# Seven-product units in both FFNs of a two-layer decoder trunk, with the down groups moved between up groups

## The chip, the core and the metric

The kernel runs on one core of a Trainium2 chip. A core has a matrix engine (TensorE, "PE" in the profile; its weight loads are "PEld"), a vector engine (VectorE, "DVE"), a scalar engine (ScalarE, "ACT"), GpSimd ("POOL") and SyncE ("SP", which here only issues DMAs). Each engine works through its own instructions in the order in which the program emitted them; semaphores make one wait for another. The metric is the device time of one execution in microseconds, as the median of several runs.

## What is computed

One sequence of 256 tokens of width 2048 goes through two layers in float32. Layer 0 has a causal pooling mixer, layer 1 a mixture of three dilated causal attentions; each is followed by a gated feed-forward network (FFN) whose up-projection passes a causal convolution of width 3. What matters here is the FFN, which both layers have:

```python
D_FF = 5504          # 43 blocks of 128

def conv_ffn(h, w_up, conv_w, conv_b, w_down):
    S = h.shape[1]
    u = h @ w_up                                   # (256, 2048) x (2048, 11008)
    up = jnp.pad(u, ((0, 0), (CONV_WIDTH - 1, 0), (0, 0)))
    c = conv_b + up[:, 0:S] * conv_w[0]
    for j in range(1, CONV_WIDTH):
        c = c + up[:, j:j + S] * conv_w[j]
    gate, val = jnp.split(c, 2, axis=-1)
    return (jax.nn.silu(gate) * val) @ w_down      # (256, 5504) x (5504, 2048)

# in each layer
h = layer_norm(ALPHA * h + mix, ln1_g[i], ln1_b[i])
ff = conv_ffn(h, ffn_w_up[i], ffn_conv_w[i], ffn_conv_b[i], ffn_w_down[i])
h = layer_norm(ALPHA * h + ff, ln2_g[i], ln2_b[i])
```

## The kernel before

**Precision.** Every large product is made of three with rounded operands: a value x is split into a high part (rounded to float32r) and a low part (the rest), and h·h, h·l and l·h are added up. The weights are split on the chip: ScalarE copies the high part (line 82), VectorE subtracts it to get the low part (line 83).

**Units.** The work is a list `units`. A unit is a block of weights, 512 x 512 as a rule (1 MB), with the function that multiplies it and one that follows it (`post`). `run_units` takes them in order. At step i it first loads ahead (`do_load`, three raw buffers) and splits ahead up to unit i+3 (`SP_AHEAD = 3`, four buffers each for high and low parts); then it emits the matmuls of unit i, then the functions whose turn has come (`later(n, fn)`: n steps from now), then the unit's own `post`. So on VectorE and ScalarE the split of unit i+3 stands ahead of what follows unit i.

**Two layouts.** In the feature-major form (`group`, `mm_quad`, lines 149 to 182) the weights are stationary and 256 tokens stream past, high and low part side by side: 16 pairs of a 512-column matmul (line 164) and a 256-column one (line 165). In the token-major form (`group_tm`, lines 188 to 268) 128 tokens are stationary and 512 columns of weights stream past: 24 matmuls (lines 230 to 232). The residual stream is feature-major in `H`; layer 1 moves it to token-major `HT` before its FFN (`to_tokens`, line 703: a transpose of 32 x 32 blocks on VectorE, then 16 DMAs for each quad of features, issued by SP).

**Seven-product units.** Some token-major units use a Strassen-like scheme: the 512 x 256 by 512 x 512 product is cut in two in each direction, and seven block products take the place of eight. Such a unit is two entries in the list, "a" (three products) and "b" (four). `split_sums` splits the block for "a", then VectorE replaces the four quarters of the raw block by their sums and differences (lines 105 to 108); for "b" ScalarE copies the changed block (line 95) and VectorE subtracts (line 96). The sums of the other operand come from `left_sums` (line 619). Products that belong to more than one quarter of the result are left in two more PSUM banks (`s2`, `s3`); `early_post` adds them up on VectorE and puts them onto `HT` with accumulating DMAs from GpSimd (line 260).

**The FFN** (`ffn`, line 556). The hidden width is cut into quads of 512 features, q = 0 to 10 (the last has 384), and these into four chunks: 0 to 2, 3 to 5, 6 and 7, 8 to 10. For each q `up` appends a gate group and a value group, four units each. After a group `evac` adds the two halves of each bank (lines 579, 580); one step later `conv` makes the first tap and the bias on ScalarE (line 588) and two taps on VectorE (line 592, eight instructions for four blocks); then come the sigmoid and the products, and the split of the result `gq[q]`. When a chunk's quads are through, `down` appends its four down groups, one for each 512 columns of the output, each with a unit for each q. FFN 0 is feature-major (`resid_add` adds to `H`; the last chunk goes through `add_last`, which also makes the layer norm's statistics). FFN 1 is token-major, and eleven of its units are seven-product units: q = 1 and q = 4 in all four groups, q = 7 in one, q = 9 in two.

Of the kernel before, what the change touches and what calls it, by code (L numbers as in the profile page):

```python
# [9 lines left out]
F32 = mybir.dt.float32  # L10
# [22 lines left out]
def trunk(ctx: ExitStack, tc: tile.TileContext, x, pool_w_in, pool_w_grp, pool_scale, pool_w_out,  # L33
# [154 lines left out]
    def group_tm(w, r0s, c0, ncol, xqs, post, apart=False, seven=None, early=None):  # L188
# [5 lines left out]
        def mk_seven(kind):  # L194
            fin = len(r0s) == 2

            def go(h, l):
                if kind == "a":
                    ps.extend([bank("s2"), bank("s3")])
                x = xqs[1]()  # L200
# [4 lines left out]
                def sm(i):  # L205
                    return lambda hl, kk: seven()[i][:, hl, kk, :]


                if kind == "a":
                    prods = [(a(0, 0), 0, N1, 2, 0, True, False), (a(2, 0), 2, N1, 0, 0, False, False),  # L210
                             (sm(3), 2, N2, 0, 1, False, fin)]
                else:
                    prods = [(a(2, 1), 2, N1, 1, 0, False, fin), (sm(2), 0, N2, 3, 0, True, False),
                             (sm(0), 0, N1, 3, 1, False, True), (sm(1), 2, N2, 2, 1, False, True)]
# [40 lines left out]
        def done():  # L255
            if not apart:
                for t in range(2):
                    post(t, ps[t])
# [3 lines left out]
        for j, (r0, nr) in enumerate(r0s):  # L262
            src = w[r0:r0 + nr, c0:c0 + ncol]
            if seven is not None and j == 1:
                units.append((src, mk_seven("a"), None, "a"))
                units.append((None, mk_seven("b"), leave if j < len(r0s) - 1 else lambda: (leave(), done()), "b"))
                continue
# [33 lines left out]

    def resid_add(c, first):
        def post(ps):
            for m in range(4):
                y = H[c][:, m, :]
                if first:
                    V.scalar_tensor_tensor(y, y, ALPHA, ps[m][:, :T], op0=OP.mult, op1=OP.add)
                else:
                    V.tensor_tensor(y, y, ps[m][:, :T], OP.add)
            for m in range(4):  # L310
                y = H[c][:, m, :]
                V.tensor_tensor(y, y, ps[m][:, T:], OP.add)
        return post
# [146 lines left out]
    def add_resid(w, rows, srcs, first):  # L460
        for c in range(4):
            group(w, rows, 512 * c, 512, srcs, resid_add(c, first))

# [70 lines left out]
    def add_grp(g):  # L534
# [12 lines left out]
             True, 0, 0)  # L547
# [8 lines left out]
    def ffn(lay):  # L556
# [3 lines left out]
        sevens = {0: (1, (0, 1, 2, 3)), 3: (4, (0, 1, 2, 3)), 6: (7, (2,)), 8: (9, (0, 2))} if lay == 1 else {}  # L560
# [133 lines left out]
        for a, b in ((0, 3), (3, 6), (6, 8), (8, 11)):  # L694
            for q in range(a, b):
                up(q)
# [410 lines left out]
```

## Time and profile before

| what | before |
|---|---|
| median of 3 runs (lowest to highest) | 2061.21 us (2060.48 to 2064.47) |
| profiled execution: span | 2060.0 us |
| around the span, against the median | 1.2 us |
| TensorE busy | 2049.6 us, 99% |
| VectorE busy | 1505.6 us, 73% |
| ScalarE busy | 1032.9 us, 50% |
| TensorE clock granted, mean | 1.000 |
| loads of weights from HBM | 380.01 MB read |

In rows of groups ("L83 DVE TENSOR_TENSOR wl<-raw,wh 128x2048 ... x325 | 743.4, 2290 | ...") stand the source line, the engine, the operation, output and inputs, the shapes and the count; then the busy time of all together in us, the mean of one in ns, and the idle time of the engine just before them with what ended it. Instructions overlap a little on one engine, so busy time over count can be less than the mean. In rows of the timeline stand the start and the length in us, and in brackets how long the engine had idled and for what it had waited. In rows of windows stand the window, its length, and the busy time of each engine in it (with the number of instructions), then the clock, the share of the DMA engines and GB/s.

### The profile page before, as it was taken

What the parts mean: (1) busy time and instruction counts of PE and PEld (TensorE: products, weight loads), DVE (VectorE), ACT (ScalarE), POOL (GpSimd) and SP (SyncE); (2) the same over time, 40 slices, a digit from 0 to 9 for tenths busy, and PEclk for the clock granted to TensorE, in tenths of its full rate; (3) what the DMA queues carried; (4) which work ended last, traced back from release to release, by engine and by line L of the source; (5) the groups of instructions that cost most, each with busy time, mean ns of one, the idle gap of its engine ahead of it and who ended that gap; (6) DMA issues with size and microseconds to landing.
All of it is one profiled execution on the core that took longest, in us unless ns stands there. A gap on an engine that the chain in (4) does not pass through costs nothing.

```text
span 2060.0 us, 29055 instructions
## 1 busy us (share of the span) xinstructions
PE 2049.6 (99%) x11942; PEld 1799.5 (87%) x11942; DVE 1505.6 (73%) x1925; ACT 1032.9 (50%) x1139; POOL 36.5 (2%) x67
## 2 busy tenths in 40 slices
PE   9999999999999999999999999999999999999998
PEld 8999988888888888889888888998888888888887
DVE  6768877756756766779755667788886787676688
ACT  6445665345534535547544344575445544544552
POOL 2000000000000000000000000000010001000000
PEclk9999999999999999999999999999999999999999
DMA  8655565655555555555566555556686558556554
GB/s 269 212 189 189 173 197 172 203 184 185 184 196 191 171 198 180 182 183 172 191 193 200 174 169 179 179 180 186 190 253 219 189 164 265 184 164 222 166 184 164
DMA packets 236997, 393.71 MB, mean 191 GB/s; under 512 B 44878, under 2 KB 56292, under 8 KB 236608
## 3 DMA queue, kind: packets, MB, share of 16 engines
q1 hardware_dynamic: 231328, 385.52, 57.4%
q0 software_dynamic: 5104, 5.69, 1.7%
q8 instruction: 93, 1.52, 0.3%
q10 hardware_dynamic: 432, 0.66, 0.1%
q14 instruction: 40, 0.33, 0.0%
HBM read 380.01 MB, written 2.10 MB: 185 GB/s over the span
## 4 chain that ended last, share of the span: by engine, by line
PE 91%; DVE 4%; DMA 2%; ACT 1%; issue 1%; SPq 0%; POOL 0%; DVEq 0%; ACTq 0%; POOLq 0%
PE acc L164 47%; PE acc L165 24%; PE t L231 3%; PE t L230 3%; PE t L232 3%; PE acc L168 3%; PE acc L169 3%; PE acc L167 3%; DVE wl L83 1%; DMA raw<-in_ffn_w_up_dram 1%; ACT wh L82 1%; DMA raw<-in_ffn_w_down_dram 1%; DMA ht<-u 0%; ACT wh L95 0%; DVE wl L96 0%
## 5 line engine op out<-in xcount | busy, mean ns | idle before, releaser
L164 PE MATMUL acc<-xc,wh 128*128 128x512 f32 x3264 | 1149.5, 396 | 0.0
L83 DVE TENSOR_TENSOR wl<-raw,wh 128x2048 fp32r<-128x2048 f32 (+2 forms) x365 | 795.5, 2184 | 405.2 <-ACT wh L82 395.5
L82 ACT CAST wh<-raw 128x2048 fp32r<-128x2048 f32 (+2 forms) x365 | 664.2, 1825 | 535.5 <-PE acc L164 346.7
L165 PE MATMUL acc<-xc,wl 128*128 128x256 f32 x3264 | 915.9, 281 | 0.0
L164 PEld LDWEIGHTS acc<-xc,wh 128*128 128x128 f32 x3264 | 615.7, 189 | 145.7 <-DVE o L959 0.6
L165 PEld LDWEIGHTS acc<-xc,wl 128*128 128x128 f32 x3264 | 615.5, 189 | 0.2
L164 PE MATMUL acc<-g,wh 128*128 128x512 f32 x644 | 226.8, 396 | 0.0
L165 PE MATMUL acc<-g,wl 128*128 128x256 f32 x644 | 180.6, 280 | 0.0
L164 PEld LDWEIGHTS acc<-g,wh 128*128 128x128 f32 x644 | 121.5, 189 | 28.4
L592 DVE SCALAR_TENSOR_TENSOR c<-u,cv,c 128x256 f32<-128x256 f32 x344 | 141.6, 478 | 0.5
L165 PEld LDWEIGHTS acc<-g,wl 128*128 128x128 f32 x644 | 121.7, 189 | 0.0
L579 ACT COPY ut<-acc 128x256 f32<-128x256 f32 x164 | 58.8, 371 | 95.7 <-PE acc L165 95.4
L231 PE MATMUL t<-wl,g 128*128 128x512 f32 (+1 forms) x267 | 102.8, 385 | 0.3 <-DVE wl L83 0.3
L230 PE MATMUL t<-wh,g 128*128 128x512 f32 (+1 forms) x267 | 103.0, 386 | 0.0
L232 PE MATMUL t<-wh,g 128*128 128x512 f32 (+1 forms) x267 | 102.6, 384 | 0.0
L588 ACT ACTIVATE c<-u,cv 128x256 f32<-128x256 f32 x172 | 89.6, 596 | 3.1 <-DVE u L580 3.1
L580 DVE TENSOR_TENSOR u<-acc,ut 128x256 f32<-128x256 f32 x164 | 60.9, 416 | 30.7 <-ACT ut L579 30.7
L164 PE MATMUL acc<-o,wh 128*128 128x512 f32 x192 | 67.9, 396 | 0.0
L164 PE MATMUL acc<-mixed,wh 128*128 128x512 f32 x192 | 67.5, 395 | 0.0
L278 ACT CAST g<-c 128x1024 fp32r<-128x1024 f32 (+1 forms) x22 | 22.6, 1029 | 84.4 <-DVE c L658 84.4
L231 PEld LDWEIGHTS t<-wl,g 128*128 128x128 f32 x267 | 50.2, 188 | 11.1 <-DVE wl L83 1.1
L232 PEld LDWEIGHTS t<-wh,g 128*128 128x128 f32 x267 | 50.1, 188 | 11.0
(265 smaller groups left out, 2358.7 us busy)
## 6 DMA issues: line engine op xcount, KB each, us to landing
raw<-in_ffn_w_up_dram SPq DMA_DIRECT2D x160, 1024.0 KB, 5.1
raw<-in_ffn_w_down_dram SPq DMA_DIRECT2D x80, 1024.0 KB, 5.1
raw<-in_pool_w_out_dram SPq DMA_DIRECT2D x16, 1024.0 KB, 5.0
raw<-in_shared_w_k_dram SPq DMA_DIRECT2D x16, 1024.0 KB, 5.1
raw<-in_attn_w_q_dram SPq DMA_DIRECT2D x16, 1024.0 KB, 5.2
raw<-in_shared_w_v_dram SPq DMA_DIRECT2D x16, 1024.0 KB, 5.8
raw<-in_attn_w_o_dram SPq DMA_DIRECT2D x16, 1024.0 KB, 5.0
raw<-in_pool_w_in_dram SPq DMA_DIRECT2D x12, 1024.0 KB, 5.7
```

Of the source, the lines that this page charges most:

```text
L82: A.copy(wh[i][:, s], r[:, s])
L83: V.tensor_tensor(wl[i][:, s], r[:, s], wh[i][:, s].bitcast(F32), OP.subtract)
L164: PE.matmul(ps[m], h[:, k, c], q[:, k, :, :T], start=st, stop=False)
L165: PE.matmul(ps[m][:, :T], l[:, k, c], q[:, k, 0, :T], start=False, stop=sp and not shifted)
L167: PE.matmul(ps[m][:, :n], h[:, k, c], q[:, k, 0, :n], start=st, stop=False)
L168: PE.matmul(ps[m][:, :n], h[:, k, c], q[:, k, 1, :n], start=False, stop=False)
L169: PE.matmul(ps[m][:, :n], l[:, k, c], q[:, k, 0, :n], start=False, stop=sp and not shifted)
L230: PE.matmul(to, xh, h[:, k, c], start=j == 0 and k == 0, stop=False)
L231: PE.matmul(to, xh, l[:, k, c], start=False, stop=False)
L232: PE.matmul(to, xl, h[:, k, c], start=False, stop=j == len(r0s) - 1 and k == nk - 1)
L588: A.activation(c[:, m, :], u[:, m, 2:], AF.Identity, scale=cv[:, 2, j:j + 1], bias=cv[:, 3, j:j + 1])
L592: V.scalar_tensor_tensor(c[:, m, :], u[:, m, i:i + T], cv[:, i, j:j + 1], c[:, m, :], op0=OP.mult, op1=OP.add)
```

## The change

1. *Order.* A chunk's four down groups no longer stand together behind its up groups. For chunks 0 and 1 the order is: gate group of the next chunk's first quad, down group 0, its value group, down group 1, gate group of the second quad, down groups 2 and 3, its value group. For chunk 2: gate 8, down 0, value 8, down 1, gate 9, down 2, value 9, down 3. The last chunk's down groups stay at the end.
2. *Seven products.* In both layers q = 1, 2, 4, 5, 6 and 7 take seven block products in all four groups (q = 9 in two, in layer 1 only): 50 units where there were 11. A group of chunk 0 or 1 is then one plain token-major unit and two seven-product units, a group of chunk 2 two seven-product units. `mk_seven` now opens and closes its banks over several units; where all units of a group are seven-product units, only half of the second token block's bank is added up.
3. *FFN 0 is token-major in its first three chunks*: `to_tokens` follows its first layer norm; behind down group 3 of chunk 2 the new `to_features` brings each quad back (a transpose on VectorE, then two times eight DMAs on SP, three steps from quad to quad), and the last chunk is feature-major as before.
4. *Taps.* `conv` makes the other two taps on ScalarE as well, four instructions each, and VectorE adds each as one whole instruction. The product of gate and value moves from the third function to the second.
5. *Memory.* Evacuation tiles are two instead of four, the buffers of the left sums change, the attention masks are made later and in shared tiles.

```diff
-            for i in (1, 0):
+            a = pools["ffn"].tile([P, 4, T], F32, name="a", tag="t4")
+            for i, to in ((1, a), (0, u[:, :, 0:T])):
                 for m in range(nb):
                     j = blk0 + m
-                    V.scalar_tensor_tensor(c[:, m, :], u[:, m, i:i + T], cv[:, i, j:j + 1], c[:, m, :],
-                                           op0=OP.mult, op1=OP.add)
+                    A.activation(to[:, m, :], u[:, m, i:i + T], AF.Copy, scale=cv[:, i, j:j + 1])
+                V.tensor_tensor(c[:, :nb], c[:, :nb], to[:, :nb], OP.add)
...
             def tmp():
-                return fp.tile([P, T], F32, name="ut", tag="t1", bufs=4)
+                return fp.tile([P, T], F32, name="ut", tag="t1", bufs=2)
...
-        sevens = {0: (1, (0, 1, 2, 3)), 3: (4, (0, 1, 2, 3)), 6: (7, (2,)), 8: (9, (0, 2))} if lay == 1 else {}
+        chunks = [(0, 3), (3, 6), (6, 8), (8, 11)]
+        order = {0: (0, 1, 2), 3: (3, 4, 5), 6: (6, 7), 8: (8, 9, 10)}
+        every = (0, 1, 2, 3)
+        sevens = {1: every, 2: every, 4: every, 5: every, 6: every, 7: every}
+        if lay == 1:
+            sevens[9] = (0, 2)
+        wait = {}
...
-        for a, b in ((0, 3), (3, 6), (6, 8), (8, 11)):
-            for q in range(a, b):
-                up(q)
-            down(range(a, b), b == 11)
+        for q in range(3):
+            up(q, (), ())
+        for n in (0, 1):
+            d = down(n, False)
+            q = chunks[n + 1][0]
+            wait[q] = sum(len(g) for g in d[1:]) + 3
+            up(q, d[:1], d[1:2])
+            up(q + 1, d[2:], ())
+            if n == 0:
+                up(q + 2, (), ())
+        d = down(2, False)
+        wait[9] = len(d[3]) - 1
+        up(8, d[:1], d[1:2])
+        up(9, d[2:3], d[3:])
+        up(10, (), ())
+        mark = len(units)
+        if lay == 0:
+            rows = [(512 * q, min(512, FF - 512 * q)) for q in (8, 9, 10)]
+            add_last(w_dn, rows, [lambda q=q: gq[q] for q in (8, 9, 10)], False, 0, 1)
+            turns(mark, 3, 3)
+        else:
+            groups = down(3, True)
+            for g in groups:
+                units.extend(g)
+            turns(mark, len(groups[0]), len(groups[1]))
...
+    def to_features(c):
+        hb = hp.tile([P, 4, T], F32, name="hb", tag="h")
+        hf = hb.rearrange("p m t -> p (m t)")
+        V.transpose(hf.rearrange("p (m t c) -> p t m c", m=4, t=2), HT[c].rearrange("p t (m c) -> p t m c", m=4))
+
+        def move(part):
+            if part == 0:
+                H[c] = hp.tile([P, 4, T], F32, name="h", tag="h")
+            to = H[c].rearrange("p m t -> p (m t)").rearrange("p (k a j) -> p a k j", k=8, a=4)
+            fr = hf.rearrange("p (k b j) -> p b k j", k=8, b=4)
+            for a in (2 * part, 2 * part + 1):
+                for b in range(4):
+                    nc.sync.dma_start(to[32 * b:32 * b + 32, a], fr[32 * a:32 * a + 32, b])
+
+        later(1, lambda: move(0))
+        later(2, lambda: move(1))
```

More of the change, by code (lines that the diff above doesn't have):

```diff
@@ L694, in ffn @@
-        for a, b in ((0, 3), (3, 6), (6, 8), (8, 11)):
-            for q in range(a, b):
-                up(q)
-            down(range(a, b), b == 11)
+            for c in range(4):
+                sv = {j: (lambda q=q: xs[q]) for j, q in enumerate(qs) if c in sevens.get(q, ())}
+                group_tm(w_dn, rows, 512 * c, 512, srcs, tm_post(lay, n, c), apart=last and c == 3,
+                         seven=sv, early=early_post(c, not last))
+                groups.append(units[mark:])
+                del units[mark:]
@@ L744, in early_post, with tm_post @@
         return post
-    def tm_post(c, first, last):
+    def tm_post(lay, n, c):
         parts = [slice(0, 256), slice(256, 512)]
+        first, last = n == 0, n == 3
         def post(t, ps, half=None):
             y = HT[c][:, t, :]
+            if lay == 0 and n == 2 and c == 3 and t == 1:
+                for q in range(4):
+                    later(1 + 3 * q, lambda q=q: to_features(q))
             if half is None and first:
```

105 lines of the change are left out of this document (45 added, 60 removed).

## The prediction

> **What bounds the kernel now.** First the page: span, busy table, clock, chain. Then the windows of the two stages that already hold seven-product units, the matmuls' timeline (to price a unit), and the timelines of VectorE and ScalarE there.
>
> ```profile
> span 2060.0 us, 29055 instructions
> PE 2049.6 (99%) x11942; PEld 1799.5 (87%) x11942; DVE 1505.6 (73%) x1925; ACT 1032.9 (50%) x1139; POOL 36.5 (2%) x67
> PEclk9999999999999999999999999999999999999999
> PE 91%; DVE 4%; DMA 2%; ACT 1%; issue 1%; SPq 0%; POOL 0%; DVEq 0%; ACTq 0%; POOLq 0%
> ```
>
> TensorE is busy 99% of the span at full clock and is 91% of the chain. Only fewer matmul columns, or fewer pauses, can make the kernel faster; and any pause adds its full length. The profiled execution's span is 2060.0 us; the median of the runs is 2061.21, so 1.2 us lie around it.
>
> Windows of layer 1's down groups of chunks 0 and 1 (span, then busy time of PE, PEld, DVE, ACT, POOL, clock, DMA share):
>
> ```profile
> 1464.00:1530.00 66.00, 64.49 (x359) 55.19 (x358) 55.32 (x63) 33.38 (x31) 7.81 (x9) 1.00 0.69 211
> 1666.00:1731.00 65.00, 65.00 (x365) 56.41 (x364) 56.53 (x64) 32.18 (x29) 7.77 (x9) 1.00 0.70 216
> ```
>
> With one seven-product unit among three, VectorE is already 84 to 87% busy there, against 73% over the span, and in the first window TensorE loses 1.51 us. That is the stage to watch.
>
> **The gain: TensorE's own work.** An up unit is 16 pairs of lines 164 and 165. A token-major unit (T) is the run of lines 230 to 232; two stand between the first two starts below, and one seven-product unit (S, entries "a" and "b") between the last two.
>
> ```profile
> L164 PE MATMUL acc<-xc,wh 128*128 128x512 f32 x3264 | 1149.5, 396 | 0.0
> 1676.91 0.40 PE L230 MATMUL t<-wh,g 128*128 128x512 f32 x1
> ...
> 1688.08 0.28 PE L219 MATMUL s<-wh,g 128*128 128x256 f32 x1
> ...
> 1693.06 0.40 PE L230 MATMUL t<-wh,g 128*128 128x512 f32 x1
> ```
>
> Each line-164 matmul overlaps the next one's start, so its busy time over its count is the pair's pitch: 1149.5/3264 = 0.352 us, and an up unit, or a feature-major down unit, is 16 x 0.352 = 5.63. T is 11.17/2 = 5.585, S is 4.98. Seven-product units go from 11 to 50: 24 in FFN 0 replace feature-major ones (24 x 0.65 = 15.6 us), 15 in FFN 1 replace T (15 x 0.605 = 9.1), and 8 units of FFN 0 become T (8 x 0.045 = 0.4). Gain 25.1 us. The 1.51 us of pauses above would go as well, as that stage is rebuilt.
>
> **The price: VectorE.** One stretch of its timeline, then ScalarE's rows and the by-shape groups.
>
> ```profile
> 1677.28 2.29 DVE L83 TENSOR_TENSOR wl<-raw,wh 128x2048 fp32r<-128x2048 f32 x1 [0.58 <-ACT wh L82]
> 1679.49 1.82 DVE L103 TENSOR_TENSOR wl<-raw,wh 128x1024 fp32r<-128x1024 f32 x2
> 1681.23 0.68 DVE L105 TENSOR_TENSOR raw<-raw 128x512 f32<-128x512 f32 x1
> ...
> 1684.01 0.42 DVE L730 TENSOR_TENSOR w<-w,s 128x256 f32<-128x256 f32 x1
> ...
> 1686.13 2.29 DVE L96 TENSOR_TENSOR wl<-raw,wh 128x2048 fp32r<-128x2048 f32 x1 [0.46 <-ACT wh L95]
> 1688.34 2.28 DVE L83 TENSOR_TENSOR wl<-raw,wh 128x2048 fp32r<-128x2048 f32 x1
> 1690.54 1.28 DVE L754 TENSOR_TENSOR ht<-ht,t 128x512 f32<-128x512 f32 x2
> 1691.74 2.28 DVE L83 TENSOR_TENSOR wl<-raw,wh 128x2048 fp32r<-128x2048 f32 x1
> 1694.59 1.83 DVE L103 TENSOR_TENSOR wl<-raw,wh 128x1024 fp32r<-128x1024 f32 x2 [0.57 <-ACT wh L101]
> 1662.91 2.29 DVE L96 TENSOR_TENSOR wl<-raw,wh 128x2048 fp32r<-128x2048 f32 x1 [2.03 <-ACT wh L95]
> ```
> ```profile
> 1655.20 1.57 ACT L101 CAST wh<-raw 128x1024 fp32r<-128x1024 f32 x2 [2.27 <-PE acc L164]
> 1666.56 0.37 ACT L579 COPY ut<-acc 128x256 f32<-128x256 f32 x1 [1.04 <-PE acc L165]
> 1666.83 2.08 ACT L588 ACTIVATE c<-u,cv 128x256 f32<-128x256 f32 x4
> 1675.34 1.91 ACT L82 CAST wh<-raw 128x2048 fp32r<-128x2048 f32 x1
> ```
> ```profile
> L592 DVE SCALAR_TENSOR_TENSOR c<-u,cv,c 128x256 f32<-128x256 f32 x344 | 141.6, 478 | 0.5
> L610 DVE TENSOR_TENSOR c<-u,c 128x1024 f32<-128x1024 f32 x20 | 24.3, 1216 | 0.5 <-ACT u L609 0.5
> L641 DVE TENSOR_TENSOR xs<-f,xs 128x256 fp32r<-128x256 f32 x14 | 5.0, 417 | 0.0
> L396 ACT ACTIVATE xp<-h,vec 128x256 fp32r<-128x256 f32 x48 | 20.4, 498 | 0.0
> L580 DVE TENSOR_TENSOR u<-acc,ut 128x256 f32<-128x256 f32 x164 | 60.9, 416 | 30.7 <-ACT ut L579 30.7
> ```
>
> From start to start: a plain split 2.21; the "a" half of a seven split 1.74 + 2.78 = 4.52 (two low parts, four subtractions in place); its "b" half 2.21; the group's posts 1.66 + 1.20 = 2.9. Between "a" and "b" ScalarE must copy the changed block (1.91), which waits for "a" and lets VectorE idle 2.03 us when nothing stands between them, 0.46 when the posts do. A taps pair costs ScalarE 8 x 20.4/48 = 3.4 us (nearest row: line 396, a copy with a per-partition scale), after four of line 588 in 2.08: its conv lasts 5.5 us instead of 2.08. VectorE gives up eight taps of 141.6/344 = 0.41 (3.3 us) and gets two whole additions like line 610's, 2.4 us.
>
> Over the whole span this fits: VectorE 1505.6 - 44 convs x 0.9 + 39 units x 4.5 + nine further sets of left sums (eight operations of 0.42 each, 30 us) is about 1670 of 2060 us, ScalarE 1032.9 + 344 x 0.425 + 39 x 1.6 about 1240. But the average isn't what decides. Two rules in the code set how far the splits may run ahead: SP_AHEAD = 3, and four weight buffers, so entry i+4 is split only after TensorE has finished entry i. A seven unit is two entries, so a lead of three entries is only 7 to 11 us of TensorE there.
>
> A *down group of chunks 0 and 1* becomes T, S, S: TensorE 5.585 + 2 x 4.98 = 15.5 us; VectorE 2.21 + 2 x 6.73 + 2.9 = 18.6, and up to 4 us of waiting for ScalarE. An up group is 22.5 us of TensorE, and some 15 of VectorE (four splits 8.8, evacuation 1.5, conv 2.4, product 1.2, half a set of sums). An up and a down group together just fit, 34 to 38 against 38. One down group between two up groups I therefore cost at nothing: the lead covers it. But groups 2 and 3 of each chunk stand side by side. Zero is the end of the up group before them; two T and two S pairs, but for the last "b", end at 31.1 - 2.8 = 28.3 us without a pause. By zero VectorE has the first three entries' splits done. Until the last "b" is split it has left, in program order: three "a" 13.6, three "b" 6.6, one T 2.2, conv 2.4, sigmoid's product 1.2, posts 2.9: 28.9 us; before the first it waits 1.6 for ScalarE (evacuation, copy), 1.0 at the "b" behind the conv, and twice 2.0 at a "b" with nothing before it: 35.5. A pause of 7.2 us, four times (two chunks, two layers): 28.8. Lower bound: only the two 2.0-us waits, 4.6 each, 18. Upper: the 4 us of waits in both groups, 9 each, 36. I take the middle, since each wait has its row.
>
> A *down group of chunk 2* is S, S: 9.95 us of TensorE. Here ScalarE's order binds. At zero the up group ends; evacuation until 0.6, the "b" copy 1.9 (its buffer comes free at zero), the conv 5.5, only then the next up unit's copy 1.9, then VectorE 2.2: 12.1, and 12.8 when VectorE is still on the "a" before, since evacuation tiles fall from four to two. So 2.5 us of pause. The next three groups start without a lead: an up and a down group ask VectorE for 8.8 + 1.5 + 2.4 + 1.2 + 13.5 + 2.6 + 5 of waits = 35 in TensorE's 32.5, so they pause longer, 3.8 by the same sum carried on. 2.5 + 3 x 3.8 = 13.9 per layer, 27.8. Bounds: 2.1 each (17), 5 each (40).
>
> **The rest.** Moves between layouts are SP's:
>
> ```profile
> 1410.87 13.34 SPq L717 DMA_DIRECT2D ht<-hb  x16
> 1424.31 1.65 SPq L72 DMA_DIRECT2D raw<-in_ffn_w_up_dram  x3
> ht<-hb SPq DMA_DIRECT2D x64, 32.0 KB, 2.0
>   DMA ht<-hb: 1.3, 1
> L260 POOL DMA_DIRECT2D ht<-u x18: 1159/1337/1519, 1494.0 to 1859.1; - x18
> ```
>
> To tokens in FFN 0 stands among up groups, as it does in layer 1, where its only trace is VectorE's 1.3 us: nothing. Back to features, each quad's 16 moves hold SP 13.3 us, land 2.0 later, and the next quad's transpose on VectorE needs that buffer; it comes every three units, of 12 x 0.352 = 4.2 in the narrow group 10, so 12.7. With the load issues that blocks VectorE's queue, splits behind it, 0 to 6 us three times; the lead there is 12.7 us. I take 2 (0 to 18). Weight loads queue behind the moves on SP, at most half a quad (6.7 us) now. POOL gets 45 more accumulating DMAs of 1.3 us on an engine 2% busy: nothing, but a group's post waits for the last one's landing if it follows closely. Left sums lie in up groups; masks move to an up group; feature-major posts (line 312) and token-major posts cost VectorE alike: nothing each.
>
> Sum: 2061.2 - 25.1 - 1.5 + 28.8 + 27.8 + 2 = **2093 us**, slower by 1.6%. With all lower bounds 2070, with all upper ones 2129.
>
> **Rivals.**
> *Faster: the lead holds.* If ScalarE runs its conv and copies ahead of VectorE, no wait adds and the pauses of chunks 0 and 1 shrink to 28.9 - 28.3 = 0.6 us each. It decides where all pauses together fall under 26.6 us, less than half of my sum. For it: up and down groups fit on average. Against: the 2.03 and 0.57 us waits are there in an easier order. Without pauses 2034.6; with chunk 2's at their lower bound and chunks 0 and 1's at 0.6, 2054. I name 2045, chance 0.24.
> *No change.* The pauses eat the gain: 2057 to 2065, 0.04.
> *The clock falls in the pauses.* Here it never did:
>
> ```profile
> 2040.00:2052.00 12.00, 11.16 (x76) 9.24 (x74) 11.57 (x23) 1.72 (x4) 1.72 (x2) 1.00 0.26 59
> ```
>
> In this window TensorE idles most of a microsecond and the granted clock stays 1.00; no row has a pause of 4 us inside the work. If each of the ten pauses of 3.8 us or more were followed by half a unit at half rate, 2.8 us each, the time is 2093 + 28 = 2121. The Trainium skill, "TensorE: Matmul & The Clock Gate", Part 1, has the array's clock halve after an idle window of about 3.4 us until as long a busy one has passed; by it each such pause would cost, as an estimate, 1.7 us more, 17 in all. The trace neither agrees nor disagrees, for want of such a pause. Chance 0.04.
> *The way back to features chokes*: 18 instead of 2, 2109, chance 0.05.
>
> **How the numbers follow.** My forecast 0.63 (its own range 2070 to 2110), the rivals as above. About 0.2%, 4 us, is what a measurement can tell. The range 2043 to 2112 leaves out half of the faster case and the clock's. Faster 0.24, same 0.04, slower 0.72.
>
> **What would show it.** After: 132 matmuls of line 164's kind on g where 644 were, and 50 x 42 of the seven products; PE's busy sum lower by about 25 us; but idle time of PE some 60 us, released by VectorE's low parts: about 7 us in groups 2 and 3 of chunks 0 and 1 in both layers, 2 to 4 behind each down group of chunk 2, where VectorE in turn waits for ScalarE's copies behind the conv. Line 592 is gone. I am wrong if VectorE is dense there and TensorE yet has no pauses (then the splits lead by more than I think), or if pauses stand at loads or transposes instead.

## The result, and the profile after

The changed kernel takes 2163.66 us as the median of four runs, beside 2061.35 for the kernel before on the same chip: a ratio of 1.0495 (95% interval 1.0481 to 1.0510). It is 102 us slower, not 32 as forecast, and outside the range, which ended at 2112. The direction and the two mechanisms that the prediction priced are in the trace; two thirds of the loss are not among its terms.

From the page of the changed kernel: span, busy table, chain, and the mean clock from the view of cores.

```profile
span 2162.9 us, 30852 instructions
PE 2068.3 (96%) x12388; PEld 1834.3 (85%) x12388; DVE 1678.5 (78%) x1971; ACT 1236.1 (57%) x1612; POOL 75.3 (3%) x112
PE 54%; DVE 20%; ACT 15%; DMA 6%; issue 5%; SPq 1%; ACTq 0%; DVEq 0%
core 0: 2162.9 us, clock 0.981
```

TensorE, 91% of the chain before, is 54% of it now; VectorE and ScalarE have 35%, and DMAs 6%. The busy sums came out as forecast (VectorE 1678.5 against "about 1670", ScalarE 1236.1 against "about 1240"), and no engine but TensorE is busy more than 78% of the span. So the loss is in waits. TensorE's busy sum must not be read as work here: it grew by 19 us although there is less to multiply, and the 30.9 us by which slow clock stretched matmuls (table below) are part of that sum.

Where TensorE waited, from its waits (us in total, times, longest):

```profile
PE acc L165 <- DVE wl L83: 22.6, 11, 2.4
PE t L223 <- ACT wh L95: 22.4, 8, 4.0
PE t L224 <- DVE wl L96: 21.2, 14, 1.9
PE acc L164 <- ACT wh L82: 5.0, 9, 1.7
PE shift L361 <- DVE S L344: 4.9, 1, 4.9
```

All but the last of these are waits for a high or a low part of weights, thus for ScalarE's copies and VectorE's splits; the last is for a sum of the layer norm at the end of FFN 0. The prediction named L96 and L83. It did not name ScalarE's copy for a "b" (L95), at 22.4 us, as something that TensorE itself waits for.

A sum over the starts of all matmuls shows where the 102.9 us of span went. Each interval from one matmul's start to the next is set against the usual interval of its kind in the same trace; what exceeds it counts as clock when it lies in a stretch of half clock, else as a pause.

| us | before | after | difference | forecast |
|---|---|---|---|---|
| matmuls at their usual pitch | 2042.6 | 2017.0 | -25.6 | -25.1 |
| pauses | 12.8 | 111.1 | +98.3 | +57 |
| matmuls stretched at half clock | 0 | 30.9 | +30.9 | 0 |
| rest (jitter both ways) | | | -0.7 | |

The pauses by place, both layers together: groups 2 and 3 of chunks 0 and 1 27.7 (forecast 28.8); around the groups of chunk 2 22.7 (forecast 27.8); the start of chunk 1's up groups and the first down group of each chunk 37.7 (forecast 0); the rest stands at the end of FFN 0 (forecast 2) and where the kernel before paused too, as at its start and in layer 1's attentions.

### The profile page after: what moved, and what is told of

The parts are those of the page before. It is cut to its first block, busy times and chain, and to the rows that moved or that the text cites. A ratio compares the mean times of both kernels' runs of the same rounds, so it can differ in the third digit from the quotient of the medians.

```text
span 2162.9 us, 30852 instructions
## 1 busy us (share of the span) xinstructions
PE 2068.3 (96%) x12388; PEld 1834.3 (85%) x12388; DVE 1678.5 (78%) x1971; ACT 1236.1 (57%) x1612; POOL 75.3 (3%) x112
## 4 chain that ended last, share of the span: by engine, by line
PE 54%; DVE 20%; ACT 15%; DMA 6%; issue 5%; SPq 1%; ACTq 0%; DVEq 0%
PE acc L164 26%; PE acc L165 13%; DVE wl L83 5%; DMA raw<-in_ffn_w_up_dram 4%; ACT wh L95 3%; ACT wh L82 3%; ACT c L585 3%; DVE wl L103 3%; DVE wl L96 2%; PE acc L169 2%; PE acc L168 2%; PE acc L167 2%; ACT a L590 2%; DMA raw<-in_ffn_w_down_dram 2%; ACT u L590 2%
## 5 line engine op out<-in xcount | busy, mean ns | idle before, releaser
L83 DVE TENSOR_TENSOR wl<-raw,wh 128x2048 fp32r<-128x2048 f32 (+2 forms) x326 | 703.1, 2170 | 236.4 <-ACT wh L82 230.2
L95 ACT CAST wh<-raw 128x2048 fp32r<-128x2048 f32 x50 | 95.3, 1906 | 167.7 <-DVE raw L108 157.3
L96 DVE TENSOR_TENSOR wl<-raw,wh 128x2048 fp32r<-128x2048 f32 x50 | 114.6, 2292 | 73.0 <-ACT wh L95 68.9
L576 ACT COPY ut<-acc 128x256 f32<-128x256 f32 x164 | 56.6, 372 | 132.2 <-DVE u L577 120.5
L224 PE MATMUL t<-wl,g 128*128 128x256 f32 x296 | 87.8, 297 | 22.8 <-DVE wl L96 21.2
L223 PE MATMUL t<-wh,g 128*128 128x256 f32 x296 | 85.6, 289 | 22.4 <-ACT wh L95 22.4
L103 DVE TENSOR_TENSOR wl<-raw,wh 128x1024 fp32r<-128x1024 f32 x100 | 91.1, 953 | 11.2 <-ACT wh L101 11.2
L101 ACT CAST wh<-raw 128x1024 fp32r<-128x1024 f32 x100 | 78.5, 834 | 33.8 <-DMA raw<-in_ffn_w_down_dram 16.8
L223 PE MATMUL s<-wh,xs 128*128 128x256 f32 x300 | 89.9, 300 | 0.0
L224 PE MATMUL s<-wl,xs 128*128 128x256 f32 x300 | 89.5, 298 | 0.0
L225 PE MATMUL s<-wh,xs 128*128 128x256 f32 x300 | 89.1, 297 | 0.0
L225 PE MATMUL t<-wh,g 128*128 128x256 f32 x296 | 85.2, 288 | 0.0
L234 PE MATMUL t<-wh,g 128*128 128x512 f32 (+1 forms) x211 | 81.2, 385 | 0.6 <-ACT wh L82 0.6
```

Source lines behind the costliest of these rows:

```text
L83: V.tensor_tensor(wl[i][:, s], r[:, s], wh[i][:, s].bitcast(F32), OP.subtract)
L95: A.copy(h, r)
L96: V.tensor_tensor(l, r, h.bitcast(F32), OP.subtract)
L103: V.tensor_tensor(l[:, k, n], r[:, k, n], h[:, k, n].bitcast(F32), OP.subtract)
L223: PE.matmul(to, xh, h[:, k, n], start=opens and kk == 0, stop=False)
L224: PE.matmul(to, xh, l[:, k, n], start=False, stop=False)
```

## The experiments

All edits are to the changed kernel unless another is named. "Lost" is the time from a group's first matmul to the next group's first, less its units at their usual price; it holds pauses and slow clock together. Ratios are to the kernel before, with their 95% intervals.

**Is it the clock?** In 18 stretches inside the work, 3.4 or 6.8 us long, the clock was half. Unread matmuls were put into the pauses, or ahead of them, to keep TensorE busy. They change no result.

```diff
+    def fill(ps, n):
+        for _ in range(n):
+            PE.matmul(ps[:, :T], neg1, XC[0][:, 0, 0, :T], start=True, stop=True)
+# 14 to 40 of them ahead of the "b" entries that wait, 16 to 30 ahead of the up groups that wait
```

> The changed kernel with matmuls that nobody reads put in front of the entries where TensorE was seen to pause over 2 us: 14 to 40 of 256 columns (0.118 us each) at the first narrow group behind chunk 0's up groups, at the 'b' entries of down groups 0 and 3, and at the up groups behind chunk 2's down groups. They fill the pauses, but leave the waits. Theory 'clock': the 19 stretches at half clock (84 us, in which matmuls took some 31 us more) come from the pauses; with TensorE kept at work they go, and the time falls by 20 to 30 us, to about 2138. Theory 'waits only': the clock's dips cost nothing of their own or come from elsewhere; the time stays at 2163 or rises by what the added matmuls overrun, to 2175.

2163.0 us (1.0487, 1.0466 to 1.0508): the time stayed, while the mean clock rose from 0.981 to 0.992. The stretches at half clock fell from 82 to 34 us and the stretched matmuls from 30.9 to 15.2 us. The pauses fell from 111.1 to 64.2, that is by 47 us, but 58 us of unread matmuls were spent on that: some 11 us of them stood in no pause and were work added, which hides most of what the clock gave back. Matched matmul by matmul with the changed kernel, this run gained 1.4 to 2.4 us at each of the four groups 3 of chunks 0 and 1 (7.5 in all), where the unread matmuls stood in the pause and no stretch of half clock was left; elsewhere it gained and lost up to some 4 us at a place. So slow clock seems to cost time of its own at least in groups 3. How much of the 30.9 us of the table would go with the clock alone, this run does not settle, as half of the slow time remained.

**Are loads late behind the layout moves?** Every second move between the layouts goes to GpSimd's queue instead of SP's, in `to_tokens` and `to_features`.

```diff
-                    nc.sync.dma_start(...)
+                    (nc.sync, nc.gpsimd)[b % 2].dma_start(...)
```

> The changed kernel, and every second move between the layouts issued by GpSimd instead of SP; nothing else. Theory 'late loads': of the pauses that I had costed at nothing, those where chunk 1's up groups begin and in the down group behind them (6.0 + 8.9 us in layer 0, 3.5 + 10.9 in layer 1), and the end of FFN 0 (8 us), come from weight loads that wait behind moves on SP's queue; half of these 37 us or more go, 2130 to 2145. Theory 'q = 2's conv': they come from conv, products and left sums of q = 2 standing right before the group; only the end of FFN 0 gains, 2153 to 2160.

2134.62 us (1.0354, 1.0333 to 1.0375): 29 us gained. The stretch before the first down group of layer 0 shows how. First the changed kernel, one fence for each engine's timeline (SP, ScalarE, TensorE):

```profile
337.63 15.55 SPq L736 DMA_DIRECT2D ht<-hb  x16
353.28 1.48 SPq L72 DMA_DIRECT2D raw<-in_ffn_w_up_dram  x1
```
```profile
359.32 1.91 ACT L82 CAST wh<-raw 128x2048 fp32r<-128x2048 f32 x1 [6.70 <-DMA raw<-in_ffn_w_up_dram]
```
```profile
371.71 0.50 PE L164 MATMUL acc<-xc,wh 128*128 128x512 f32 x1 [1.70 <-ACT wh L82]
374.65 0.58 PE L165 MATMUL acc<-xc,wl 128*128 128x256 f32 x1 [2.43 <-DVE wl L83]
...
399.22 0.58 PE L223 MATMUL t<-wh,g 128*128 128x256 f32 x1 [3.95 <-ACT wh L95]
```

Then the same moves with the queue split (SP, GpSimd, ScalarE):

```profile
333.19 8.21 SPq L736 DMA_DIRECT2D ht<-hb  x8
```
```profile
333.73 4.61 POOL L736 DMA_DIRECT2D ht<-hb  x8 [11.26 <-DVE u L577]
```
```profile
347.47 1.91 ACT L82 CAST wh<-raw 128x2048 fp32r<-128x2048 f32 x1 [1.62 <-PE acc L164]
```

The 16 moves of one quad held SP for 15.55 us, the weights behind them came late, and ScalarE idled 6.70 us for a load; TensorE stood still only 10 to 40 us later, when the lead of three entries had been used up. With the queue split the copy waits for TensorE instead, that is, for a free buffer: the lead is whole. What was lost at the start of chunk 1's up groups went from 6.0 and 3.5 us (layer 0 and 1) to 0, in the first down group of chunk 0 from 8.9 and 10.9 to 3.8 each, at the end of FFN 0 from 8.0 to 1.8: 27.9 of the 29 us.

What was left in the first down groups, 3.8 us, has a row too. ScalarE's and VectorE's timelines of the run with the split queue, in the first down group:

```profile
380.97 2.09 ACT L585 ACTIVATE c<-u,cv 128x256 f32<-128x256 f32 x4
...
386.16 1.90 ACT L95 CAST wh<-raw 128x2048 fp32r<-128x2048 f32 x1
```
```profile
388.10 2.29 DVE L96 TENSOR_TENSOR wl<-raw,wh 128x2048 fp32r<-128x2048 f32 x1 [0.44 <-ACT wh L95]
```

The copy for the "b" stands behind the 5.2 us of the conv, its split ends at 390.4, and TensorE waits for it:

```profile
390.44 0.38 PE L224 MATMUL t<-wl,g 128*128 128x256 f32 x1 [1.95 <-DVE wl L96]
```

The next two runs take ScalarE's order apart.

**Is it ScalarE's taps?** First the two taps go back to VectorE.

```diff
-            for i, to in ((1, a), (0, u[:, :, 0:T])):
+            for i in (1, 0):
                 for m in range(nb):
                     j = blk0 + m
-                    A.activation(to[:, m, :], u[:, m, i:i + T], AF.Copy, scale=cv[:, i, j:j + 1])
-                V.tensor_tensor(c[:, :nb], c[:, :nb], to[:, :nb], OP.add)
+                    V.scalar_tensor_tensor(c[:, m, :], u[:, m, i:i + T], cv[:, i, j:j + 1], c[:, m, :],
+                                           op0=OP.mult, op1=OP.add)
```

> One part undone: the two other taps are VectorE's again, eight instructions of 0.41 us, no whole additions. VectorE gets 0.9 us more per conv (40 us in all), ScalarE 3.4 us less. Theory 'ScalarE's order': the pauses behind chunk 2's down groups (23 us in both layers) and at the first up group behind chunk 0 (4.6 and 3.4 us) come from a conv of 5.5 us standing before the next copy on ScalarE; they shrink to less than half and the time falls to 2125 to 2145. Theory 'VectorE's sum': VectorE's work as such sets the pauses; they grow by 10 to 20 us, and the time is 2170 to 2185.

2136.6 us (1.0359, 1.0338 to 1.0380): 27 us gained, in the range of the theory of ScalarE's order, although VectorE has more to do. In layer 0 the loss before chunk 1's up groups fell from 6.0 to 0.2, in the first down group of chunk 1 from 3.8 to 0, in chunk 2's first group from 5.9 to 1.4. In groups 2 and 3 it stayed (10.3 and 9.7, before 9.8 and 8.6), and in chunk 0's first group it rose from 8.9 to 10.7.

But the theory had the pauses behind chunk 2's down groups shrink to less than half, and they didn't: TensorE's idle time in the eight up groups there (both layers) was 19.6 us in the changed kernel and 17.3 here. VectorE's and TensorE's timelines of this run show why: the taps now stand on VectorE, ahead of the low part that TensorE waits for.

```profile
800.14 3.25 DVE L589 SCALAR_TENSOR_TENSOR c<-u,cv,c 128x256 f32<-128x256 f32 x8
...
804.56 2.28 DVE L83 TENSOR_TENSOR wl<-raw,wh 128x2048 fp32r<-128x2048 f32 x1
```
```profile
806.90 0.39 PE L165 MATMUL acc<-xc,wl 128*128 128x256 f32 x1 [3.23 <-DVE wl L83]
```

Second, the taps stay with ScalarE, but the last one, with the product behind it, is emitted one step later, so that copies can come between.

```diff
-            for i, to in ((1, a), (0, u[:, :, 0:T])):
-                ...
+            tap(c, u, cv, 1, pools["ffn"].tile([P, 4, T], F32, name="a", tag="t4"), blk0, nb)
+        # the caller, one step on:
+            later(1, half)      # half: last_tap(c, u, ...), the product, then later(..., three)
```

> The changed kernel with each conv spread over two steps: bias and first two taps in one, the last tap (and what follows) one step later, so that the next unit's copy on ScalarE waits for 3.8 us of conv instead of 5.5. No work is added or taken away. Theory 'ScalarE's order': the pauses behind chunk 2's down groups (23 us) fall to under 12, and the time to 2140 to 2152. Theory 'VectorE's sum': the same work in the same lead; 2160 or more.

2146.53 us (1.0409, 1.0388 to 1.0430): 17 us gained with the same instructions on the same engines, only in another order. It is not simply a part of the 27, as it comes in part from other places: TensorE's idle time in chunk 2's eight up groups fell from 19.6 to 10.6 us, where the taps on VectorE left 17.3. The rows of the changed kernel behind a group of chunk 2 show the wait in full (ScalarE, then TensorE):

```profile
804.36 0.70 ACT L576 COPY ut<-acc 128x256 f32<-128x256 f32 x2 [2.86 <-DVE u L577]
805.00 1.91 ACT L95 CAST wh<-raw 128x2048 fp32r<-128x2048 f32 x1
806.81 2.08 ACT L585 ACTIVATE c<-u,cv 128x256 f32<-128x256 f32 x4
808.79 1.70 ACT L590 ACTIVATE a<-u,cv 128x256 f32<-128x256 f32 x4
810.39 1.70 ACT L590 ACTIVATE u<-u,cv 128x256 f32<-128x256 f32 x4
811.99 1.90 ACT L82 CAST wh<-raw 128x2048 fp32r<-128x2048 f32 x1
```
```profile
813.95 0.50 PE L164 MATMUL acc<-xc,wh 128*128 128x512 f32 x1 [0.28 <-ACT wh L82]
816.86 0.39 PE L165 MATMUL acc<-xc,wl 128*128 128x256 f32 x1 [2.42 <-DVE wl L83]
```

Evacuation, "b" copy, conv, only then the next unit's copy: the sequence that the prediction laid out, with 5.2 us of conv where it had 5.5.

**Is it the evacuation tiles?** ScalarE waited 120.5 us for them in the changed kernel (line 576, for VectorE's line 577). A third tile, in memory shared with the masks' tiles:

```diff
-                return fp.tile([P, T], F32, name="ut", tag="t1", bufs=2)
+                return fp.tile([P, T], F32, name="ut", tag="t1", bufs=3)
```

> Three evacuation tiles instead of two (four don't fit in memory). ScalarE was seen waiting 120 us in all for VectorE to free such a tile, 42 times. Theory 'lead': VectorE is the one that is late, so ScalarE's wait only shows it; less than 8 us change, 2155 to 2164. Theory 'tiles': ScalarE's blocked copies make VectorE late in turn; 15 to 30 us less, 2133 to 2148.

2156.61 us (1.0456, 1.0435 to 1.0477): 7 us. ScalarE's waits, changed kernel first:

```profile
ACT ut L576 <- DVE u L577: 120.5, 42, 7.5
```
```profile
ACT ut L576 <- DVE u L577: 70.1, 30, 5.8
```

50 us less waiting of ScalarE, 7 us less time: most of that wait is off the path, and the two tiles are a small cause.

**Did the new order help or harm?** The down groups stand together behind their chunk again; the 50 seven-product units stay.

```diff
-        for q in range(3):
-            up(q, (), ())
-        for n in (0, 1):
-            d = down(n, False)
-            ...
+        for n in range(3):
+            for q in range(*chunks[n]):
+                up(q, (), ())
+            for g in down(n, False):
+                units.extend(g)
```

> One part undone: a chunk's down groups stand together behind its up groups again; 50 seven-product units, taps on ScalarE and the layout as in the changed kernel. Theory 'lead': the order is worth something, as an up group between two down groups lets VectorE catch up: together, four groups of chunk 2 ask VectorE for 20 us in TensorE's 10 each. Time 2180 to 2215. Theory 'order is worthless': VectorE's total per chunk decides, or the new order brings the pauses itself: 2164 or less.

2241.14 us (1.0868, 1.0846 to 1.0890), clock 0.962: 77 us slower than the changed kernel, more than either theory gave. The pauses grew to 164 us. The interleaving is worth a great deal; it is the 50 units that cost.

**Two seven-product units in a group, or one?** One of them becomes a plain unit: 26 where there were 50.

```diff
-        sevens = {1: every, 2: every, 4: every, 5: every, 6: every, 7: every}
+        sevens = {1: every, 4: every, 7: every}
```

> Fewer seven-product units: q = 1, 4, 7 in both layers (and q = 9 in two groups of layer 1), 26 instead of 50; order, taps and layout as in the changed kernel. A down group then asks VectorE for 15 us in TensorE's 16. Theory 'lead': pauses in down groups 2 and 3 of chunks 0 and 1 (7 us each), in group 0 of each chunk and behind chunk 2's groups nearly vanish, with them the half clock; what stays is the start of chunk 1's up groups (4 us in each layer) and the way back to features (8 us). TensorE's work is 10.6 us less than before: 2052 to 2070. Theory 'order': the interleaved order itself or the taps on ScalarE cost; over 2085.

2078.73 us (1.0083, 1.0066 to 1.0100): 85 us gained, although TensorE's work rises by 14.0 (2031.0 against 2017.0). The pauses fall from 111 to 31.5 us and the stretched matmuls to 7.8. It came out above the range for the lead and below the bound of the rival; the pauses left were at the start of chunk 1's up groups (4 us in each layer), at the end of FFN 0 (9) and in layer 1's last chunk (4), none of them at groups 2 and 3.

**The same with the taps on VectorE**, and then with the buffer of the way back to features taken from two pools in turn:

```diff
-        hb = hp.tile([P, 4, T], F32, name="hb", tag="h")
+        pool, tag = (lnp, "sq") if c % 2 else (hp, "h")
+        hb = pool.tile([P, 4, T], F32, name="hb", tag=tag)
```

> 26 seven-product units (q = 1, 4, 7, and 9 in part) and the taps on VectorE again. With one_seven 2078.7: its pauses at the start of chunk 1's up groups (3.9 and 4.1 us) should vanish as they did with the taps back alone, and with them most of the half clock; what stays is the way back to features (8.8 us) and the last chunk in layer 1. Theory 'two causes that add': 2062 to 2070. Theory 'with little VectorE work the taps cost nothing': 2076 to 2080.

> As one_seven_taps, and the way back to features uses two buffers in turn, so that VectorE's transpose no longer waits for the moves before it (7.3 us in two waits in the changed kernel). Theory: the pauses there come from VectorE's blocked queue; they shrink from 8.8 to under 4, 2056 to 2065, about 5 us under one_seven_taps. Rival: they come from the weight loads that queue behind the moves on SP, which stay; within 2 us of one_seven_taps.

2060.06 us (0.9991, 0.9981 to 1.0000) with the taps, better than expected; 18.7 us of gain. With the second buffer 2060.45 (0.9992, 0.9983 to 1.0002): nothing. One pause was left, 7.6 us at the end of FFN 0, and the buffer isn't its cause. ScalarE's and SP's timelines there, in the run with one buffer:

```profile
898.20 1.91 ACT L82 CAST wh<-raw 128x2048 fp32r<-128x2048 f32 x1 [5.31 <-DMA raw<-in_ffn_w_down_dram]
```
```profile
886.16 6.57 SPq L754 DMA_DIRECT2D h<-hb  x8
892.83 1.09 SPq L72 DMA_DIRECT2D raw<-in_ffn_w_down_dram  x2
895.43 6.44 SPq L754 DMA_DIRECT2D h<-hb  x8
```

The loads stand between the moves on SP. So the split of the queue was tried on this kernel too, the taps once on VectorE and once on ScalarE:

> one_seven_taps (2060.1) with every second move between the layouts issued by GpSimd instead of SP, for both ways. There the last pause of 7.5 us in FFN 0 goes with weight loads that ScalarE waits for (4.5, 1.8 and 5.3 us) while SP issues moves. Theory 'SP's queue': the loads come in time, the pause shrinks to under 3 us, time 2052 to 2056. Theory 'the transposes': VectorE is held by the moves' landing, which GpSimd's slower issue only delays; 2060 or more.

> one_seven_queues (2048.05) with the taps on ScalarE as in the changed kernel. With a free SP queue and one seven-product unit in a group neither engine is pressed. Theory 'the taps only cost where the lead is gone': within 3 us of one_seven_queues, 2046 to 2051. Theory 'ScalarE's conv always costs': 2055 to 2067, as one_seven stood 18.7 us above one_seven_taps.

2048.05 us (0.9933, 0.9918 to 0.9948) and 2056.53 us (0.9971, 0.9962 to 0.9981). The first is the lowest time of all, 0.67% under the kernel before. Groups 2 and 3 of layer 0's chunk 0, with the up groups around them, in its windows (TensorE, weight loads, VectorE, ScalarE, GpSimd, clock, DMA share, GB/s):

```profile
441.00:530.00 89.00, 89.00 (x506) 77.42 (x505) 70.53 (x98) 45.80 (x47) 5.68 (x8) 1.00 0.64 203
```

TensorE is busy without a gap, VectorE 79%. The taps on ScalarE cost 8.5 us here, 18.7 before the split of the queue (2078.73 to 2060.06) and 27 with 50 units. Read together: the less lead there is, the more ScalarE's long conv costs.

**Groups 2 and 3 side by side.** Group 3 was moved behind the second quad's value group, with 50 units and the taps on VectorE.

```diff
-            wait[q] = sum(len(g) for g in d[1:]) + 3
+            wait[q] = sum(len(g) for g in d[1:]) + 7
+            wait[q + 1] = len(d[3]) - (n == 0)
             up(q, d[:1], d[1:2])
-            up(q + 1, d[2:], ())
+            up(q + 1, d[2:3], d[3:])
```

> taps_back (2136.6) with 50 seven-product units, and one thing more: down groups 2 and 3 of chunks 0 and 1 no longer stand side by side, group 3 comes behind the second quad's value group. Theory 'lead': the pauses in group 3 (7.6 us four times, 30 in all) come from two groups in a row without an up group between them; at most 8 of them stay, and the time is 2105 to 2118. Theory 'VectorE's average': the same work has to be done in the same stretch, the pauses move into the groups that stand alone; over 2125.

2124.86 us (1.0304, 1.0283 to 1.0325): 11.7 better than with the taps alone; less than the theory of the lead gave, and a hair short of the rival's bound. Windows of the two groups with what lies between them, taps alone first, then apart (in the second an up group of 22.5 us stands between):

```profile
462.00:504.00 42.00, 35.16 (x221) 31.82 (x220) 35.60 (x45) 20.05 (x21) 2.85 (x4) 0.92 0.49 151
```
```profile
463.00:521.00 58.00, 55.48 (x349) 50.13 (x348) 52.36 (x73) 30.54 (x32) 3.06 (x5) 0.98 0.53 169
```

TensorE's idle share in this place fell from 6.8 us of 42 to 2.5 of 58. In layer 0 the two groups lost 4.1 (chunk 0) and 2.7 us (chunk 1) instead of 10.3 and 9.7, but chunk 2's first group now lost 8.7 instead of 1.4, as group 3 of chunk 1 stands nearer to it. So the mechanism holds at its place, and half of its gain moved on. With 26 units there is nothing to gain by it:

> one_seven_queues with down groups 2 and 3 apart, too. Theory 'lead': with one seven-product unit in a group, VectorE's 15 us fit in TensorE's 16 and nothing pauses there; within 2 us of one_seven_queues. If a pause hid there, faster by more.

2048.55 us (0.9935, 0.9919 to 0.9952).

**All remedies together, with 50 units** (queue split, taps on VectorE, group 3 apart):

> 50 seven-product units with the taps on VectorE, down groups 2 and 3 apart, and the moves shared by SP and GpSimd: all that helped, at the changed kernel's number of units. apart_two_seven took 2124.9, with pauses and slow clock of 16 us around chunk 0's first group in layer 0, 11 in layer 1, 8 at the end of FFN 0, some 34 in chunk 2's groups. Theory 'VectorE's work in chunk 2's groups stays': 2085 to 2105, still slower than before. Theory 'the late loads were behind it all': under 2060.

2091.94 us (1.0147, 1.0127 to 1.0167). Windows of chunk 0's first two down groups with the up groups behind them, first in the changed kernel, then in this one, with chunk 2's first three down groups and the up groups behind them as a second row:

```profile
381.50:467.00 85.50, 78.90 (x475) 69.90 (x473) 70.52 (x75) 48.96 (x60) 5.23 (x6) 0.96 0.60 195
```
```profile
375.00:452.00 77.00, 76.32 (x473) 67.92 (x472) 66.31 (x79) 40.56 (x41) 5.24 (x6) 1.00 0.65 205
733.60:848.00 114.40, 103.49 (x640) 92.73 (x640) 99.94 (x124) 60.37 (x65) 7.77 (x9) 0.96 0.58 184
```

The same groups take 77.0 us where they took 85.5, with TensorE busy 99%: what was lost in the first down groups is 0.1 us each. Chunk 2 still loses: VectorE is busy 87% there, and 54.7 us of pauses stand in the whole span. Fifty units remain too many for VectorE and ScalarE, whatever the order tried here.

**FFN 1 alone.** The kernel with 26 units and the taps on VectorE, but FFN 0 feature-major as before, without seven products:

```diff
-        sevens = {1: every, 4: every, 7: every}
+        sevens = {1: every, 4: every, 7: every} if lay == 1 else {}
+# layer 0: up groups, then resid_add groups, chunk by chunk, as before; no to_tokens, no to_features
```

> one_seven_taps with FFN 0 feature-major in the old order without seven-product units, as before the change: no way to tokens and back there. TensorE has 12 seven-product units less (0.65 us each) and 16 plain ones 0.05 longer, 8.6 us; the pauses of FFN 0 (9 us) and its half clock (3 us) go. Theory: both cancel, 2056 to 2060, so that FFN 0's token-major form is worth what its way back costs. Against one_seven_queues it should be slower by the 8 us of TensorE's work if that one has lost its pause.

2059.67 us (0.9987, 0.9977 to 0.9996). With the moves on SP alone, a token-major FFN 0 brings TensorE some 10 us (2041.1 to 2030.8 at the usual pitch) and gives all of it back (2060.06 beside 2059.67). With the queue split it is 11.6 us better than this (FFN 1 alone with the split wasn't run).

## Why the prediction was wrong

*Right: the gain.* TensorE's work fell by 25.6 us, forecast 25.1, from three pitches and three counts.

*Right: groups 2 and 3 side by side.* Four pauses of 6.3 to 7.3 us, 27.7 in all; forecast 4 x 7.2 = 28.8. (With the slow clock around them some 37 us were lost there.) TensorE's and VectorE's timelines in layer 0's chunk 0 have them in three parts, behind the "a" and "b" entries that were computed:

```profile
495.05 0.39 PE L224 MATMUL s<-wl,g 128*128 128x256 f32 x1 [0.89 <-DVE wl L103]
...
500.44 0.43 PE L223 MATMUL t<-wh,g 128*128 128x256 f32 x1 [3.11 <-ACT wh L95]
...
502.77 0.58 PE L224 MATMUL t<-wl,g 128*128 128x256 f32 x1 [1.90 <-DVE wl L96]
```
```profile
488.80 2.29 DVE L96 TENSOR_TENSOR wl<-raw,wh 128x2048 fp32r<-128x2048 f32 x1 [2.03 <-ACT wh L95]
...
500.42 2.29 DVE L96 TENSOR_TENSOR wl<-raw,wh 128x2048 fp32r<-128x2048 f32 x1 [2.04 <-ACT wh L95]
```

Both 2.0-us waits of VectorE at a "b" with nothing ahead of it are there. The run with group 3 apart confirms the place.

*Right in mechanism, somewhat large: chunk 2.* 22.7 us of pauses, forecast 27.8, in the sequence quoted above. The conv in two steps supports it (19.6 to 10.6 us of TensorE's idle time there). The taps on VectorE alone do not remove these pauses (17.3), as the conv then stands ahead of the low part on the other engine.

*Wrong: "One down group between two up groups I therefore cost at nothing: the lead covers it."* These places lost 37.7 us in pauses, about 47 with the clock. The balance of 34 to 38 us of VectorE against 38 of TensorE was right (VectorE is busy 70.52 us over two such pairs in the changed kernel's window above), but it took for granted that the group starts with the full lead. It didn't, for the reason of the step that failed with it: **"To tokens in FFN 0 stands among up groups, as it does in layer 1, where its only trace is VectorE's 1.3 us: nothing"**, and "Weight loads queue behind the moves on SP, at most half a quad (6.7 us) now", which holds for the way back alone: on the way to tokens all 16 moves of a quad still stood ahead of the loads. Nor was VectorE's 1.3 us the only trace that the moves left in layer 1. ScalarE, too, idled behind them in the kernel before, for loads:

```profile
1429.83 1.91 ACT L82 CAST wh<-raw 128x2048 fp32r<-128x2048 f32 x1 [5.82 <-DMA raw<-in_ffn_w_up_dram]
1448.41 1.91 ACT L82 CAST wh<-raw 128x2048 fp32r<-128x2048 f32 x1 [5.72 <-DMA raw<-in_ffn_w_up_dram]
```

What TensorE lost there was small (1.51 us in the window from 1464 us), and so the moves were read as being free; they were covered by the lead, ahead of down groups with one seven-product unit and with a conv of 2.08 us on ScalarE. The moves are no dearer in the changed kernel (16 of them held SP 10.4 to 15.6 us, 10.4 to 16.1 before); their cover is gone. Two pairs of runs show by what. With the moves on SP and the taps on VectorE, layer 0's first down group lost 10.7 us with two seven-product units in a group and 1.1 with one. The start of chunk 1's up groups lost its 6.0 us in layer 0 only where late loads and ScalarE's long conv came together: either the split of the queue or the taps on VectorE took it away, so the gains of these two runs don't add up. ScalarE's waits for up-projection weights, in the kernel before and in the changed one:

```profile
ACT wh L82 <- DMA raw<-in_ffn_w_up_dram: 36.9, 12, 5.8
```
```profile
ACT wh L82 <- DMA raw<-in_ffn_w_up_dram: 141.5, 46, 7.3
```

The moves are only a part of this sum: with the queue split it is still 113.2 us, so the sum by itself says little of the loss. Splitting the queue gained 29 us, 28 of them at these places and at the end of FFN 0. The second part of this miss is that a "b" copy behind the conv was priced in chunk 2 but not in the first down groups, where it costs 3.8 us with the clock (with queue and taps both mended: 0.1).

*Wrong: the way back to features at 2 us.* 8.0 were lost there, inside its bounds of 0 to 18, but not by the wait that the step priced. It had the next quad's transpose wait for its buffer and hold up VectorE's queue; a second buffer gained nothing (tried with 26 units). The loads behind the moves on SP were the cause: with the queue split 1.8 us were left.

*Wrong in kind: the clock as a rival with a chance of 0.04.* It wasn't another way in which things could go; it came with pauses such as the forecast itself had. It stretched matmuls by 30.9 us, near the 28 that the rival gave. The sum had no term for it. How much of it is a cost of its own, beside the pauses, the run with the pauses filled leaves open.

Forecast and measured, in pauses: 57 against 98; the 38 us of the first groups, 6 more at the end of FFN 0 and 5 less in chunk 2 make nearly all of the difference. The range failed for the same reason: its upper bounds moved each priced wait and left the terms costed at nothing at nothing; even all of them together gave 2129.

Open: what slow clock costs by itself, what else than the conv sets the pauses of chunk 2, and whether 50 units could pay with another division of the splits between the engines, which wasn't tried.

## What to carry to other kernels

A resource that is hidden in the kernel before is hidden by a lead, and a change that uses up the lead must be charged for everything which the lead covered, the transfers on the issuing queue first. Count what stands ahead of a copy on its in-order engine at each place where a group waits, not only at the place where the sum of work is tightest: the engine with 57% busy time set part of these waits, and 27 us went with its taps. Where matrix work is traded for vector work, try half of it: 26 units instead of 50 kept 12 of the 26 us and, with the queue split, gave the lowest time, under both kernels (2048.05 us).

## What the runs showed of the hardware

*The clock fell after short pauses.* In the kernel before, the clock inside the work stayed at full; TensorE idled there for 1.81 us at the longest. In the changed kernel 18 stretches of 3.41 or 6.83 us had half clock. One began 0.7 us behind a single pause in which TensorE idled 1.94 us; pauses with 1.83 us of idle, at 851 us, and with 2.43 us, at 1537 us, left the clock alone. So the length of a pause did not decide it by itself. TensorE's timeline at the first (matmuls 0.12 us apart, then 0.21), and the pause of 2.43 us with the window around it, where the granted clock stayed 1.00:

```profile
612.60 0.39 PE L224 MATMUL t<-wl,g 128*128 128x256 f32 x1 [1.94 <-DVE wl L96]
...
613.17 0.32 PE L225 MATMUL t<-wh,g 128*128 128x256 f32 x1
613.29 0.41 PE L223 MATMUL s<-wh,xs 128*128 128x256 f32 x1
613.50 0.41 PE L224 MATMUL s<-wl,xs 128*128 128x256 f32 x1
```
```profile
1539.93 0.39 PE L165 MATMUL acc<-xc,wl 128*128 128x256 f32 x1 [2.43 <-DVE wl L83]
```
```profile
1538.00:1545.00 7.00, 5.07 (x29) 4.42 (x30) 6.97 (x9) 5.58 (x8) 0.00 (x0) 1.00 0.44 150
```

The Trainium skill, "TensorE: Matmul & The Clock Gate", Part 1, has the clock halve after an idle window of about 3.4 us. The length of the stretches agrees with that window; that a pause of about 2 us was once enough does not, and the measurement decides.

*Two queues issued the small moves sooner than one.* In the quad shown above sixteen moves of 32 KB held SP 15.55 us; split, eight held SP 8.21 us and eight held GpSimd 4.61 us at the same time. Which of the two, the time of an issue or the order behind it, the loads gain from was not told apart.
